# One slot more in a ring of weight chunks, one split buffer fewer of each kind

## The chip, the cores and the metric

The kernel runs on one core of one Trainium2 chip. The metric is the device time of a launch in microseconds, median over the runs. One further execution was taken with the hardware profiler, and every row shown here comes from that one.

## The reference, cut to what matters

One layer of a decoder trunk on 512 tokens of width 1024, in float32. A token mixer (three groups of heads: a convolution, a gated recurrence, chunked linear attention) is followed by a mixture of 16 experts in 4 groups: each token takes the best group and in it the best two experts. The change touches only how the weights of the experts are held, so only that part is shown.

```python
def hier_moe(h, w_rg, b_rg, w_re, b_re, w_gate, w_up, w_down):
    ...
    for g in range(N_GROUPS):
        a = jnp.einsum("bsd,edf->bsef", h, w_gate[g])
        up = jnp.einsum("bsd,edf->bsef", h, w_up[g])
        hid = jax.nn.silu(a) * up * comb[:, :, g, :, None]
        y = y + jnp.einsum("bsef,efd->bsd", hid, w_down[g])
    return y

def reference(...):
    ...
        x = x + gt1 * token_mix(h, ...)
        h = rms_norm(x, g_ffn[l]) * (1.0 + sc2) + sh2
        x = x + gt2 * hier_moe(h, ...)
    return rms_norm(x, g_final)
```

With `D_MODEL = 1024` and `D_EXPERT = 512`, each expert has three matrices of 2 MB, so the 16 experts have 96 MB, and all of it is read.

## The kernel before

The first half of the time goes to the token mixer and the routing. Behind it stands the unit loop over the experts, about 262 to 525 us of the profile. The kernel gathers the tokens of an expert (at most 128), multiplies, and adds the results back to the rows in memory.

**Units.** Eight units (0 to 7) hold one expert each, with up to 128 tokens; the code calls them `alone(u)`. Four units (8 to 11) hold two experts each, with up to 64 tokens apiece, in the two halves of the array. In the order of the program, unit u does its gate product, the transposes of the hidden rows of unit u-1, its up product, the transposes of the gathered rows of unit u+1, and then the down product of unit u-1 (`whole`), whose result is scaled by `gt2` (tile `ye`) and scattered.

**Chunks.** Each matrix is loaded in two chunks of 1 MB (`load_chunk`, line 964), 96 chunks in all, in the order of use: gate, up, and the down of the unit before. A chunk lives in a slot of the ring: chunk `i` in slot `i % nring`. `nring` is 17: 13 slots from pools that are opened as earlier stages end, and four of the pool `ring2`, which takes the place of the mixer's last tiles. A load waits for its slot to be free of the chunk `nring` back, and for the load three before it, so that three are on the way at a time. All loads go through SP's queue, in order. Nine chunks are loaded while the mixer still runs, three more behind its projections, four as the routing ends, and `for i in range(HELD + 1, nring)` loads those that are left ahead of the unit loop.

**Splits.** In the single-expert units the product is made in three parts of reduced precision. A chunk is taken in two halves, called quarters (of a matrix). For each quarter ScalarE casts the weights (line 87, tile `mh`), and VectorE subtracts the cast from the weights (line 88, tile `ml`):

```python
        hi = mw.tile([P, k // 4, 4096 // k], F32R, tag="mh", name=f"mh_{name}{s}")
        lo = mw.tile([P, k // 4, 4096 // k], F32R, tag="ml", name=f"ml_{name}{s}")
        split(hi, lo, raw[:, s * (k // 4):(s + 1) * (k // 4), :])
        if s:
            load_chunk(i + nring)
```

TensorE then does two triples per quarter in `mm3`: line 82 (cast weights, cast rows), line 83 (remainder of the weights), line 84 (cast weights, remainder of the rows). The pool `mw` has three buffers of `mh` and three of `ml`, 4 KB a partition each. A new tile in a buffer waits for every reader of the old one. When the second quarter of a chunk is split, the slot is free and the next load is traced. In the down product the last quarter is used as it is, unsplit (line 1449, four matmuls), in all single-expert units but 3 and 7 (`full(u)`).

The paired units use the chunks straight from the ring (lines 1412 and 1458), with no split; a slot is free once its matmuls are done.

**Order.** The program is written in the order above, and at build time the framework makes from it one list per engine, by priority and its own estimates of when an operand is there. In the trace the lists mix neighbouring units: a one-hot product of a later unit stands between two subtractions, transposes of gathered rows between two quarters of a down. At run time each engine goes through its list in order and waits where it must.

**The tail.** When the chunks are through, `slot` goes on in the same ring for seven more tiles (two with split results, four with rows of the output, one with the final scale).

Of the kernel before, what the change touches and what calls it, by code (L numbers as in the profile page):

```python
# [42 lines left out]
EARLY = 12  # L43
# [3 lines left out]
def trunk_kernel(  # L47
# [105 lines left out]
    rings = []  # L153

    def add_ring(n, name, side="right"):
        pool = ctx.enter_context(tc.tile_pool(name=name, bufs=n, side=side, reuse_waits="tile"))
        rings.extend([pool] * n)
        return pool
# [785 lines left out]
                              for s in range(2) for c in cols_of(n))  # L944
    picked = {}
    raws = {}
    nring = len(rings) + 4

    loads = []

# [4 lines left out]
    def load_chunk(i, *first):  # L955
        if i >= len(chunks):
            return
        w, c, k, s, _, name = chunks[i]
        raw = rings[i % nring].tile([P, k // 2, 4096 // k], F32, tag="raw", name=f"raw_{name}")
        if c >= NS and c not in picked:  # L960
            picked[c] = nc.values_load(ranked[0:1, c - NS:c - NS + 1], engines=[mybir.EngineType.SP],
                                       min_val=NS, max_val=NE - 1)
        src = w[c:c + 1] if c < NS else w[bass.ds(picked[c], 1)]
        d = nc.sync.dma_start(raw, src.rearrange("e (p k) n -> p (e k) n", p=P)[:, s * (k // 2):(s + 1) * (k // 2), :])

        if len(loads) >= AHEAD:
            after(d, loads[-AHEAD])
        for other in first:
            after(d, other)
        loads.append(d)  # L970
        raws[i] = raw

    for i in range(nring - 8):
        load_chunk(i)

    def yres(i, half, ps):
# [48 lines left out]
    def route(i):  # L1025
        route_half(i, 1)
        nc.sync.dma_start(xo_dram[i * P:(i + 1) * P, :], xt[i])
        junk = late.tile([P, D], BF16, tag="junk2", bufs=1, name=f"junk2{i}")
        nc.scalar.activation(junk, xt[i], AF.Square, accum_out=ss2[:, i:i + 1])
        rstd_of(ss2[:, i:i + 1], ss2[:, i:i + 1], D)  # L1030
        pl2 = small(f"pl2{i}")
        for hf in range(2):
            nc.tensor.matmul(pl2[:, 0:20], pls[i, hf], sel, start=(hf == 0), stop=(hf == 1))
        nc.vector.scalar_tensor_tensor(lg[:, i, :], pl2[:, 0:20], ss2[:, i:i + 1], lgc, ALU.mult, ALU.add)
# [13 lines left out]
    for i in range(2):  # L1048
        yres(i, 1, py[i])
    py = project((2, 3), [lambda i=i: [route_half(n, 0) for n in (i, i + 1)] for i in (0, 2)]  # L1050
                 + [lambda i=i: route(i) for i in (0, 1)])
    for i in range(nring - 8, EARLY):
        load_chunk(i)
    for i in (0, 1):
        rows(i)
# [11 lines left out]
    for g in gat:  # L1067
        nc.gpsimd.memset(g, 0.0)
    lts.close()
    add_ring(4, "ring2", side="left")  # L1070
    mw = ctx.enter_context(tc.tile_pool(name="mw", bufs=3, reuse_waits="tile"))
    hpool = ctx.enter_context(tc.tile_pool(name="hot", bufs=4, reuse_waits="tile"))

    shalf = hpool.tile([P, 2 * (NU - NS - NB)], U32, bufs=1, name="shalf")
# [591 lines left out]
```

## Time and profile before

| | us |
|---|---|
| median of 3 runs | 544.43 |
| the three runs | 543.29 to 544.66 |
| the profiled execution, own time | 542.79 |
| its span (first to last instruction) | 541.1 |
| busy in the span: TensorE | 509.2 |
| VectorE | 362.6 |
| ScalarE | 248.4 |
| GpSimd | 90.4 |

The span is what the trace shows; the 1.7 us between it and the execution's own time lie around it. Engines are called PE (TensorE), PEld (its weight loads), DVE (VectorE), ACT (ScalarE), POOL (GpSimd) and SP, whose queue issues the loads. Busy time is a sum over the whole span: a stage in which an engine is full and one in which it is idle come out as one share. Matmuls are pipelined, so one lasts longer in the record than the distance to the next.

### The profile page before, as it was taken

To read this page: it belongs to the slowest core of one execution; us is meant where nothing else is said; L and a number is where in the kernel's file an instruction comes from. 1 tells how busy PE (TensorE), PEld (TensorE's weight loads), DVE (VectorE), ACT (ScalarE), POOL (GpSimd) and SP (SyncE) were. 2 spreads that over 40 slices of the span, in tenths; PEclk is the share of its full clock that TensorE was granted. 3 is DMA by queue.
4 is the path that set the end of the run, shared out by engine and by line. 5 is a ranking of instruction groups with operands and counts; after the bars stand their busy time and mean duration, and the time that the engine had idled before them with its cause. 6 is when DMAs were issued, how large, how long until landed. Compare 5 with 4: busy or idle time off the path is not lost.

```text
span 541.1 us, 7963 instructions
## 1 busy us (share of the span) xinstructions
PE 509.2 (94%) x2835; PEld 344.8 (64%) x2835; DVE 362.6 (67%) x654; ACT 248.4 (46%) x397; POOL 90.4 (17%) x126
## 2 busy tenths in 40 slices
PE   8999999999989999997889999999999999999891
PEld 7766766677657887766668777787876443342341
DVE  4544499999988747448799999999897121020227
ACT  5432587496126533334457768676774110000103
POOL 3311424000025100104110220120222010211002
PEclk9999999999999999996699999999999999999996
DMA  8995978748818399379899899999999999999963
GB/s 284 302 345 160 273 259 269 249 164 303 274 60 303 124 395 421 115 265 313 297 329 327 316 377 364 353 365 382 353 373 377 367 403 366 402 368 375 391 252 155
DMA packets 54304, 164.58 MB, mean 304 GB/s; under 512 B 12181, under 2 KB 30881, under 8 KB 39926
## 3 DMA queue, kind: packets, MB, share of 16 engines
q1 hardware_dynamic: 50710, 156.36, 78.9%
q0 software_dynamic: 3552, 7.69, 5.4%
q8 instruction: 23, 0.38, 0.3%
q14 instruction: 19, 0.16, 0.1%
HBM read 156.35 MB, written 12.62 MB: 312 GB/s over the span
## 4 chain that ended last, share of the span: by engine, by line
PE 28%; DMA 16%; DVE 5%; issue 1%; ACT 0%; POOL 0%; POOLq 0%; DVEq 0%; SPq 0%
DMA raw_u<-in_w_up_dram 7%; DMA raw_d<-in_w_down_dram 6%; DMA raw_g<-in_w_gate_dram 3%; PE pga L84 2%; PE pga L83 2%; PE pga L82 2%; PE pup L83 2%; PE pup L84 2%; PE pup L82 2%; PE pd L82 2%; PE pd L1449 2%; PE pd L83 2%; PE pd L84 2%; PE pd L1458 2%; PE pgt L1381 2%; PE pga L1412 1%
## 5 line engine op out<-in xcount | busy, mean ns | idle before, releaser
L507 DVE SCALAR_TENSOR_TENSOR cacc<-upad,vt,cacc 128x512 f32<-128x512 f32 x60 | 43.1, 755 | 0.1
L1536 DVE SCALAR_TENSOR_TENSOR sact<-pup,swt,sact 128x512 f32<-128x512 f32 x12 | 8.9, 745 | 50.1 <-PE pup L1412 50.1
L88 DVE TENSOR_TENSOR ml_u<-raw_u,mh_u 128x1024 fp32r<-128x1024 f32 x32 | 39.1, 1224 | 3.9 <-ACT mh_u L87 3.7
L87 ACT CAST mh_g<-raw_g 128x1024 fp32r<-128x1024 f32 x32 | 33.4, 1051 | 16.9 <-PE pga L84 12.3
L88 DVE TENSOR_TENSOR ml_g<-raw_g,mh_g 128x1024 fp32r<-128x1024 f32 x32 | 38.3, 1219 | 1.3 <-ACT mh_g L87 1.1
L87 ACT CAST mh_u<-raw_u 128x1024 fp32r<-128x1024 f32 x32 | 33.6, 1049 | 11.6 <-PE pga L84 9.4
L1458 PE MATMUL pd<-raw_d,ht 128*64 128x512 f32 x128 | 35.0, 600 | 1.5 <-DMA raw_d<-in_w_down_dram 1.5
L88 DVE TENSOR_TENSOR ml_d<-raw_d,mh_d 128x1024 fp32r<-128x1024 f32 x26 | 31.7, 1222 | 4.0 <-ACT mh_d L87 3.6
L1140 POOL DMA_INDIRECT gat<-h_rows,sidx x12 | 13.5, 1122 | 121.1 <-PE pgt L1381 68.9
L87 ACT CAST mh_d<-raw_d 128x1024 fp32r<-128x1024 f32 x26 | 27.3, 1049 | 8.1 <-PE pup L84 6.1
L1412 PE MATMUL pup<-raw_u,xh 128*64 128x512 f32 x128 | 29.4, 595 | 1.2 <-DMA raw_u<-in_w_up_dram 1.2
L1486 DVE TENSOR_TENSOR ye<-pd,gt 128x512 f32<-128x512 f32 x22 | 15.0, 690 | 21.8 <-PE pd L1458 20.3
L1412 PE MATMUL pga<-raw_g,xh 128*64 128x512 f32 x128 | 28.3, 594 | 0.0
L82 PE MATMUL pga<-mh_g,xh 128*128 128x512 f32 x64 | 27.4, 428 | 0.5 <-ACT xh L87 0.5
L83 PE MATMUL pup<-ml_u,xh 128*128 128x512 f32 x64 | 25.6, 400 | 1.6 <-DVE ml_u L88 1.5
L83 PE MATMUL pga<-ml_g,xh 128*128 128x512 f32 x64 | 26.1, 408 | 1.0 <-DVE ml_g L88 1.0
L84 PE MATMUL pga<-mh_g,xl 128*128 128x512 f32 x64 | 25.5, 399 | 0.4 <-DVE xl L88 0.4
L82 PE MATMUL pup<-mh_u,xh 128*128 128x512 f32 x64 | 25.8, 403 | 0.0
L84 PE MATMUL pup<-mh_u,xl 128*128 128x512 f32 x64 | 25.2, 394 | 0.0
L1458 PEld LDWEIGHTS pd<-raw_d,ht 128*64 128x64 f32 x128 | 10.8, 136 | 21.4 <-issue 16.8
L1084 POOL DMA_INDIRECT xo_rows<-ye,sidx x8 | 17.1, 2138 | 36.8 <-DVE ye L1486 36.8
L1424 ACT COPY ht<-pht 128x512 f32<-128x512 f32 x4 | 2.3, 586 | 43.0 <-PE pht L1420 43.0
(405 smaller groups left out, 1270.1 us busy)
## 6 DMA issues: line engine op xcount, KB each, us to landing
raw_g<-in_w_gate_dram SPq DMA_DIRECT2D x32, 1024.0 KB
raw_u<-in_w_up_dram SPq DMA_DIRECT2D x32, 1024.0 KB
raw_d<-in_w_down_dram SPq DMA_DIRECT2D x32, 1024.0 KB
wb<-in_w_ada_dram SPq DMA_DIRECT2D x16, 1024.0 KB
wa<-in_w_ada_dram SPq DMA_DIRECT2D x8, 512.0 KB
wa<-in_w_ada_dram SPq DMA_DIRECT2D x4, 1024.0 KB
raw_o<-in_w_out_dram SPq DMA_DIRECT2D x8, 512.0 KB
xin<-in_x_dram SPq DMA_DIRECT2D x4, 512.0 KB
```

The lines of the kernel that those rows point to most:

```text
L82: nc.tensor.matmul(ps, lh, rh, start=start, stop=False)
L83: nc.tensor.matmul(ps, lh, rl, start=False, stop=False)
L84: nc.tensor.matmul(ps, ll, rh, start=False, stop=stop)
L87: one = nc.scalar.copy(hi, src)
L88: two = nc.vector.tensor_tensor(lo, src, hi.bitcast(F32), ALU.subtract)
L507: nc.vector.scalar_tensor_tensor(cacc[:, h, :], upad[:, h, t:t + T], w, cacc[:, h, :], ALU.mult, ALU.add)
L1084: nc.gpsimd.indirect_dma_start(out=xo_dram, out_offset=bass.IndirectOffsetOnAxis(ap=si, axis=0), in_=y, in_offset=None, bounds_check=T - 1 ...
L1140: return g, nc.gpsimd.indirect_dma_start(out=g, out_offset=None, in_=h2_dram, in_offset=bass.IndirectOffsetOnAxis(ap=sidx[:, e:e + 1], axi ...
L1381: nc.tensor.transpose(pt[:, kk * P:(kk + 1) * P], gv[:, :, k], ident)
L1412: nc.tensor.matmul(ps[rows_of(a)], xh[:, k, rows_of(a)], raws[used[0] + a][:, kk, :], start=(k == 0), stop=(k == KD - 1))
L1458: nc.tensor.matmul(ps[hf][rows_of(a)], ht[:, k, rows_of(a)], raws[used[0] + k // 2 * 2 + a][:, k % 2, cols(hf)], start=(k == 0), stop=(k = ...
L1486: nc.vector.tensor_tensor(y[:, cols], ps[hf], gt2[:, cols], ALU.mult)
```

## The change

The ring gets an eighteenth slot: `ring2` has five slots, not four. Two numbers that are worked out from `nring` are set so that the same nine and three chunks as before are loaded ahead of the routing. The room of 8 KB a partition comes from the pool `mw`: two buffers of `mh` and two of `ml`, not three.

```diff
-    nring = len(rings) + 4
+    nring = len(rings) + 5
...
-    for i in range(nring - 8):
+    for i in range(nring - 9):
         load_chunk(i)
...
-    for i in range(nring - 8, EARLY):
+    for i in range(nring - 9, EARLY):
         load_chunk(i)
...
-    add_ring(4, "ring2", side="left")
-    mw = ctx.enter_context(tc.tile_pool(name="mw", bufs=3, reuse_waits="tile"))
+    add_ring(5, "ring2", side="left")
+    mw = ctx.enter_context(tc.tile_pool(name="mw", bufs=2, reuse_waits="tile"))
```

## Rows read from the trace of the kernel before

**Rows 1.** The page, busy time, share and instructions of each engine.

```profile
PE 509.2 (94%) x2835; PEld 344.8 (64%) x2835; DVE 362.6 (67%) x654; ACT 248.4 (46%) x397; POOL 90.4 (17%) x126
```

**Rows 2.** Windows: length, busy PE, PEld, DVE, ACT, POOL, granted clock, DMA share, GB/s.

```profile
300.00:310.00 10.00, 10.00 (x44) 7.66 (x43) 9.27 (x10) 6.88 (x9) 2.36 (x1) 1.00 0.88 304
...
440.00:450.00 10.00, 10.00 (x50) 3.48 (x46) 0.00 (x0) 1.08 (x2) 0.00 (x0) 1.00 1.01 372
...
490.00:500.00 10.00, 8.75 (x40) 2.77 (x36) 0.18 (x1) 0.60 (x1) 1.55 (x1) 1.00 1.02 374
...
500.00:510.00 10.00, 8.95 (x34) 3.18 (x34) 1.35 (x5) 0.59 (x1) 0.00 (x0) 1.00 1.02 378
```

**Rows 3.** The chain that ended last: start us, us, what.

```profile
299.76 1.72 PE pd L1449 x4
...
352.52 0.90 PE pgt L1381 x8
...
413.74 1.72 PE pd L1449 x4
...
504.47 7.80 DMA raw_d<-in_w_down_dram
```

**Rows 4.** Waits of SP's queue, 283 to 415 us: us in total, times, longest.

```profile
SPq L964 <- DMA raw_g<-in_w_gate_dram: 26.7, 13, 3.8
...
SPq L964 <- DVE ml_g L88: 10.9, 8, 2.5
```

**Rows 5.** Waits of SP's queue, 414 to 418 us.

```profile
SPq L964 <- PE pd L1449: 2.5, 1, 2.5
```

**Rows 6.** Groups by form, 283 to 415 us: busy us, mean ns of one.

```profile
L84 PE MATMUL pga<-mh_g,xl 128*128 128x512 f32 x56 | 22.2, 397 | 0.4 <-DVE xl L88 0.4
...
L82 PE MATMUL pd<-mh_d,hh 128*128 128x512 f32 x44 | 17.8, 411 | 0.0
...
L1486 DVE TENSOR_TENSOR ye<-pd,gt 128x512 f32<-128x512 f32 x13 | 8.8, 689 | 0.4 <-PE pd L1449 0.2
...
L1536 DVE SCALAR_TENSOR_TENSOR sact<-pup,swt,sact 128x512 f32<-128x512 f32 x7 | 5.2, 742 | 0.0
...
L1535 ACT ACTIVATE sact<-pga 128x512 f32<-128x512 f32 x7 | 4.2, 601 | 0.0
...
L1226 DVE TENSOR_TENSOR ohs<-iota,pos 128x512 bf16<-128x512 f32 x4 | 2.7, 687 | 0.0
```

**Rows 7.** Timeline, 273 to 277 and 323 to 325 us: start us, us, engine, what.

```profile
273.10 1.22 DVE L88 TENSOR_TENSOR ml_u<-raw_u,mh_u 128x1024 fp32r<-128x1024 f32 x1
...
274.37 0.50 PE L83 MATMUL pup<-ml_u,xh 128*128 128x512 f32 x1 [1.54 <-DVE ml_u L88]
...
275.42 0.40 PE L84 MATMUL pup<-mh_u,xl 128*128 128x512 f32 x1
...
275.85 1.05 ACT L87 CAST mh_u<-raw_u 128x1024 fp32r<-128x1024 f32 x1 [1.97 <-PE pup L84]
...
276.93 1.23 DVE L88 TENSOR_TENSOR ml_u<-raw_u,mh_u 128x1024 fp32r<-128x1024 f32 x1
...
323.04 0.39 PE L82 MATMUL pga<-mh_g,xh 128*128 128x512 f32 x1
...
324.44 0.39 PE L82 MATMUL pga<-mh_g,xh 128*128 128x512 f32 x1
```

**Rows 8.** Waits of ScalarE's casts, 283 to 415 us: us in total, times, longest.

```profile
ACT mh_g L87 <- PE pga L84: 12.3, 7, 2.1
...
ACT mh_u L87 <- PE pga L84: 7.4, 20, 0.7
...
ACT mh_d L87 <- PE pup L84: 6.1, 17, 0.7
```

**Rows 9.** Issues of loads, size of one.

```profile
raw_g<-in_w_gate_dram SPq DMA_DIRECT2D x32, 1024.0 KB
```

**Rows 10.** Window of 2 us in unit 0, columns as in rows 2.

```profile
272.00:274.00 2.00, 0.83 (x11) 0.36 (x9) 2.00 (x3) 1.54 (x2) 0.00 (x0) 1.00 0.96 360
```

## The prediction

> **What bounds the kernel now.** I read the page first [rows 1]: TensorE is busy 94% of the span. That is an average over stages, so the windows come next [rows 2]. In the stage of the whole-unit experts (units 1 to 7, about 283 to 415 us) TensorE is busy for the whole of 10 us at the full granted clock, VectorE for 9.27 of them, and the transfers for 88%: three resources close to full at once. In the stage of the paired experts, behind 415 us, VectorE is nearly idle and the transfers run at a share of about 1 (372 GB/s); TensorE is full there too but for the last 20 us, in which it waits some 2.3 us. The chain of waits [rows 3] goes through matmuls up to 415.5 us and in the paired stage through transfers of weights, the last until 512.3 us. So the end is set by the weight stream and by TensorE together, and both enter the paired stage when the first stage lets them.
>
> That the stream can't run on by itself is in the waits of SP's queue. In the first stage [rows 4] a load most often waits for an earlier one (13 times for a gate load, 26.7 us), but 8 times for ml_g, the subtraction that ends the use of a gate chunk. Where the stages meet [rows 5] it waits for line 1449's matmuls, 2.5 us: there the ring is full, and a later end of unit 7 holds back the stream.
>
> The groups by form [rows 6] give the work of that stage: 56 matmuls of line 84 for gate, as many for up and 44 for down, two to a quarter, so 28 + 28 + 22 = 78 quarters. The groups of line 1449 (1.72 us for four) that end the downs of units 0 and 6 start at 299.76 and 413.74 us [rows 3], six periods apart: 19.0 us a unit. Quarters follow each other in 1.40 us (323.04 to 324.44, [rows 7]). Eleven of them make 15.4, line 1449 1.7, transposes and one-hot products the rest, about 1.8.
>
> **The change, part by part.**
>
> *Two split buffers of each kind, not three.* Follow one set of buffers in the timeline [rows 7]. A subtraction on VectorE starts at 273.10 and takes 1.22, to 274.32; the second matmul of that quarter, which needs it, starts at 274.37, 0.05 later. The sixth starts at 275.42 and ends at 275.82. ScalarE starts the cast that uses the set next at 275.85, named as released by that matmul; it takes 1.05, and its subtraction starts at 276.93, 0.03 behind its end, and takes 1.23. Once round: 0.03 + 1.05 + 0.03 + 1.23 + 0.05 + 1.45 (second matmul's start to sixth's end) = 3.84 us. A set must go round once in as many quarters as there are sets. With three, TensorE's pace gives 3 x 1.40 = 4.20: 0.36 to spare. The waits say how near the limit that is: 44 of the 78 casts (7 + 20 + 17) waited for just this last matmul [rows 8]. With two, the pace gives 2.80 and the loop still wants 3.84, so the loop becomes the bound: 1.92 us a quarter, not 1.40. What hid the 2.4 us of cast and subtraction was two further quarters of matmuls (2.80); one (1.40) doesn't.
>
> Behind the waiting cast on ScalarE stand the copy of the transposed hidden rows, the SiLU and the casts of the gathered rows; VectorE's product of SiLU and up waits for those, and TensorE's transposes and downs for that.
>
> Now one unit. *Lower end*: 11 x 1.92 = 21.1; line 1449 makes its pair of quarters 2.80 + 1.72 = 4.52, 0.7 over the loop; the other TensorE work fits gaps of 0.52. 21.8 us, 2.8 more than now. The one unit of the seven whose down is split in all four quarters (down 3) wants 12 x 1.92 = 23.0, 4.0 more. Sum 6 x 2.8 + 4.0 = 20.8. *With today's order kept* I carried the loop through a unit by hand. VectorE does the scaled output (2 x 0.69) ahead of the third gate subtraction, a one-hot (0.69) ahead of the fourth, the product with up (0.74) ahead of the third down; ScalarE does copy and SiLU (0.60) ahead of the last up cast; TensorE does eight transposes (0.90, [rows 3]) ahead of the second down quarter. Counted from the end of line 1449, the second matmuls fall at 0.23, 1.63, 3.96, 5.88, 7.85, 9.71, 11.57, 13.71, 15.51, 17.80, 19.81, and the next unit's first at 23.03: 22.8 us, 3.9 more than the 18.9 that the same count gives for now. For the full unit it gives 23.8, 5.0 more. Sum 6 x 3.9 + 5.0 = 28.4. *Upper end*: of VectorE's 5 us of other work in a unit about 1 falls on the loop in this count; if half did, a unit takes 24.3, and seven 5.4 each, 38. The build orders each engine's list anew, so a better fit may take some of the 28.4 back. I take **26**, nearer to the order seen than to the floor.
>
> *Units 0 and 7.* In unit 0 (262 to 282 us) VectorE also sorts the tables and is the bound; the loop's gap lies partly under that. Zero to 4 us; I take **2**. Two quarters of down 7 fall into the paired stage, and wait about 1 us each there; zero where the stream is the bound, 2 where TensorE is; I take **1**.
>
> *The eighteenth slot.* The loads ahead of the unit loop are the same and one more; from then on a load waits for the chunk 18 back. Where the stages meet, the stream is one chunk further. A chunk is 1024 KB [rows 9]; at 372 GB/s that is 2.8 us less to move in the paired stage. Nothing, if TensorE fills that time by itself; at most about 2.8, since TensorE has but 2.3 us of idle time there [rows 2] and little behind. I take **-2.8**. Slack of the transfers in the slower first stage gives no more: a load needs a slot.
>
> *The rest.* The loads' kinds and their order stay, and so does the computation; the tail takes its tiles from ring slots in rotation, one slot earlier than now. Nothing, with the last stage's transfers as cover; if a tail tile came behind the last down, a us or two.
>
> Sum: 26 + 2 + 1 - 2.8 = 26.2. The profiled execution took 542.8 us (its span 541.1 and 1.7 around it): 569.0. The median of the runs shown stands 1.6 above that execution, so I say **570 us**.
>
> **The rivals.**
>
> *A. Two sets are enough, and the slot gains.* The split of the next quarter goes on under the matmuls of this one, and the stream's lead of a chunk comes out at the end: 542.8 - 2.8 = 540, or 542 as a median. It decides if the loop is under 2.80 us. For it: ScalarE and VectorE have idle time in each quarter. Against it: cast and subtraction alone take 2.28, which leaves 0.5 for the matmuls between. The Trainium skill, in Trainium Kernel Development and Optimization, Best Practices, says to double-buffer for performance. Read as "two will do" it gives this rival's time; rows 7 and 8 speak against it. 4%.
>
> *B. The build interleaves better.* If all other TensorE work (3.5 us a unit) and all of VectorE's fits the gaps, a unit takes 21.1: 7 x 2.1 - 2.8 = 12 more, or 556. If matmuls of other units stepped into the gaps too, some 3 to 10 more. For it: today's lists mix units. Against: with two sets only two quarters are ready at a time, of whichever unit. 10%, with a tenth of that inside 0.3%.
>
> *C. The clock falls.* With a gap in every quarter the granted clock may go to 0.5, the 1.2 GHz level. Matmuls would then start 0.47 apart, and a unit take some 35 us; over half of the stage that is 43 us more, about 613 with the rest. Against it: at 272 to 274 us TensorE was busy for 0.83 of 2 us and the granted clock was 1.00 [rows 10]. The Trainium skill, TensorE: Matmul & The Clock Gate, A second HAM failure mode, tells of short idles between groups of matmuls that make the clock swing; row 10 shows such a stall without it. 4%.
>
> **How the numbers follow.** My forecast, +12 to +39 by the bounds above, has 82%; B 10% and A 4% lie below it, C 4% above. The range for 8 in 10 goes from the case in which the gaps take up all other work (556) to the upper end (38 + 4 - 2.8 = 39, 584). Within 0.3% (1.6 us, about what a measurement here can tell from no change): 3%. Faster: 3%, all of it A. Slower: 94%.
>
> **What would show it.** Line 1449's groups 22 to 23 us apart; nearly all 78 casts released by a matmul; TensorE idle for about half a us ahead of most second matmuls, released by the subtraction; the transfers' share in that stage near 0.8, with SP waiting for subtractions; the paired stage as long as now or up to 3 us shorter; the clock at 1.00. I'd be wrong if line 1449's groups stayed 19 us apart (A), or if the paired stage were 10 us or more shorter and gave the loss back.

## The result and the profile after

| | us |
|---|---|
| before, median of 3 runs | 544.43 |
| after, median of 3 runs | 567.85 (567.34 to 568.54) |
| ratio, 95% interval | 1.0441 [1.0408, 1.0473] |
| profiled execution after, own time | 567.34 |
| its span | 565.4, before 541.1 |

Slower by 4.4%, 23.4 us on the median and 24.3 us on the span; 570 us was forecast, between 556 and 584. The chain of waits after answers to [rows 3]: start us, us, what.

```profile
304.25 1.72 PE pd L1449 x4
...
395.20 1.72 PE pd L1449 x4
...
436.05 1.00 PE pga L1412 x2
...
437.72 1.01 PE pga L1412 x4
...
441.24 1.72 PE pd L1449 x4
...
528.21 8.35 DMA raw_d<-in_w_down_dram
```

The first and the last group of line 1449 stand at 304.25 and 441.24 us, 137.0 us apart where it was 114.0: a unit takes 22.8 us, not 19.0. The first group is 4.5 us late, the last 27.5, the end of the span 24.3. So all of the loss is made up to 441 us, and 3.2 us come back in the paired stage. The windows of the two stages, before and then after (columns as in [rows 2]):

```profile
283.00:415.00 132.00, 131.93 (x670) 103.09 (x669) 122.76 (x144) 95.19 (x111) 21.56 (x13) 1.00 0.97 357
415.00:512.00 97.00, 94.51 (x442) 36.64 (x440) 16.81 (x32) 8.72 (x15) 10.43 (x7) 1.00 1.00 381
```

```profile
283.00:443.00 160.00, 148.08 (x679) 102.23 (x680) 123.12 (x144) 95.88 (x112) 20.11 (x14) 1.00 0.89 304
443.00:536.00 93.00, 93.00 (x434) 35.90 (x434) 17.84 (x32) 9.99 (x16) 10.44 (x7) 1.00 0.99 376
```

VectorE does the same 123 us of work in the first stage, over 160 us where it was 132; no engine is full there, and the transfers fall from a share of 0.97 to 0.89. The paired stage is as before, but TensorE no longer has idle time in it. What the first stage waits for is in the timeline, which answers to [rows 7]:

```profile
287.07 1.05 ACT L87 CAST mh_g<-raw_g 128x1024 fp32r<-128x1024 f32 x1 [1.24 <-PE pga L84]
...
288.15 1.23 DVE L88 TENSOR_TENSOR ml_g<-raw_g,mh_g 128x1024 fp32r<-128x1024 f32 x1 [0.91 <-ACT mh_g L87]
...
289.43 0.50 PE L83 MATMUL pga<-ml_g,xh 128*128 128x512 f32 x1
...
290.47 0.40 PE L84 MATMUL pga<-mh_g,xl 128*128 128x512 f32 x1
...
290.91 1.05 ACT L87 CAST mh_u<-raw_u 128x1024 fp32r<-128x1024 f32 x1 [1.38 <-PE pga L84]
...
293.27 0.50 PE L83 MATMUL pup<-ml_u,xh 128*128 128x512 f32 x1 [0.33 <-DVE ml_u L88]
...
294.74 1.05 ACT L87 CAST mh_u<-raw_u 128x1024 fp32r<-128x1024 f32 x1 [0.94 <-PE pup L84]
```

Read it as a circle: cast at 287.07, its subtraction at 288.15, the second matmul at 289.43, the sixth at 290.47, and the next cast on that set at 290.91, released by it: 3.84 us. The next turn ends at 294.74, 3.83 us on. Each step of the circle starts 0.03 to 0.05 us behind the end of the step before it. The groups of waits say how often an engine stood still for that, between 283 and 442 us (us in total, times, longest):

```profile
PEld pup L83 <- DVE ml_u L88: 16.3, 25, 1.1
ACT mh_g L87 <- PE pga L84: 14.6, 13, 2.1
...
ACT mh_u L87 <- PE pga L84: 10.7, 13, 1.4
ACT mh_g L87 <- PE pd L84: 9.6, 12, 1.6
ACT mh_u L87 <- PE pup L84: 9.2, 11, 1.2
...
PEld pd L83 <- DVE ml_d L88: 6.1, 12, 1.0
ACT mh_d L87 <- PE pup L84: 5.0, 7, 0.9
...
ACT mh_d L87 <- PE pd L84: 4.3, 3, 2.8
PEld pga L83 <- DVE ml_g L88: 4.0, 10, 0.8
```

59 of 78 casts wait for a sixth matmul, 53.4 us in all. That count by itself says little: with three sets 55 casts did (the 44 of [rows 8] and two groups that aren't shown there), for 29.7 us:

```profile
ACT mh_g L87 <- PE pd L84: 3.2, 9, 0.6
...
ACT mh_d L87 <- PE pd L84: 0.7, 2, 0.3
```

What is new is on TensorE. Before 47 of the 78 quarters its weight load waits for a subtraction, 26.4 us, near the 27.5 us that are lost up to the last group; with three sets that were 3 waits and 0.9 us. (While a load waits, earlier matmuls still run: the matmuls themselves stand idle for a subtraction 30 times, 10.2 us.) On SP's queue, in the same stretch, the loads that in [rows 4] mostly waited for an earlier load now wait for subtractions:

```profile
SPq L964 <- DVE ml_u L88: 45.1, 14, 3.7
SPq L964 <- DVE ml_g L88: 28.5, 10, 4.1
SPq L964 <- DVE ml_d L88: 27.4, 12, 4.4
...
SPq L964 <- DMA raw_g<-in_w_gate_dram: 1.1, 2, 0.9
```

The ring is full nearly throughout: an eighteenth slot in it holds a chunk that nobody is ready to use.

### The profile page after: what moved, and what is told of

Read it like the earlier page. It is cut to its first block, busy times and chain, and to the rows that moved or that the text cites. A ratio compares the mean times of both kernels' runs of the same rounds, so it can differ in the third digit from the quotient of the medians.

```text
span 565.4 us, 7966 instructions
## 1 busy us (share of the span) xinstructions
PE 523.2 (93%) x2835; PEld 341.5 (60%) x2835; DVE 363.1 (64%) x654; ACT 248.8 (44%) x397; POOL 87.6 (15%) x126
## 4 chain that ended last, share of the span: by engine, by line
PE 30%; DVE 11%; ACT 5%; DMA 5%; issue 1%; POOL 0%; POOLq 0%; DVEq 0%; SPq 0%; ACTq 0%
PE pga L1412 4%; PE pd L1458 4%; PE pup L1412 4%; DMA raw_d<-in_w_down_dram 3%; DVE ml_u L88 3%; DVE ml_d L88 3%; DVE ml_g L88 2%; PE pga L83 2%; PE pd L83 2%; PE pup L83 2%; ACT mh_u L87 2%; PE pd L1449 2%; PE pga L84 2%; ACT mh_g L87 2%; PE pd L84 2%; PE pgt L1381 2%
## 5 line engine op out<-in xcount | busy, mean ns | idle before, releaser
L83 PE MATMUL pup<-ml_u,xh 128*128 128x512 f32 x64 | 28.4, 444 | 7.5 <-DVE ml_u L88 7.4
L1084 POOL DMA_INDIRECT xo_rows<-ye,sidx x8 | 15.7, 1958 | 117.2 <-DVE ye L1486 117.2
L1412 PE MATMUL pga<-raw_g,xh 128*64 128x512 f32 x128 | 30.6, 595 | 0.0
L83 PE MATMUL pga<-ml_g,xh 128*128 128x512 f32 x64 | 28.0, 437 | 2.5 <-DVE ml_g L88 2.1
L83 PE MATMUL pd<-ml_d,hh 128*128 128x512 f32 x52 | 22.0, 423 | 2.4 <-DVE ml_d L88 2.2
L83 PEld LDWEIGHTS pup<-ml_u,xh 128*128 128x128 f32 x64 | 12.0, 187 | 19.3 <-DVE ml_u L88 17.7
```

The lines of the kernel that those rows point to most:

```text
L83: nc.tensor.matmul(ps, lh, rl, start=False, stop=False)
L1084: nc.gpsimd.indirect_dma_start(out=xo_dram, out_offset=bass.IndirectOffsetOnAxis(ap=si, axis=0), in_=y, in_offset=None, bounds_check=T - 1 ...
L1412: nc.tensor.matmul(ps[rows_of(a)], xh[:, k, rows_of(a)], raws[used[0] + a][:, kk, :], start=(k == 0), stop=(k == KD - 1))
```

## The experiments

Each ratio below is against the kernel before as measured beside that run; its median was 544.03, 544.69 or 545.66 us.

**Is it the split buffers or the slot?** The two parts of the change, apart. First the buffers alone:

```diff
-    mw = ctx.enter_context(tc.tile_pool(name="mw", bufs=3, reuse_waits="tile"))
+    mw = ctx.enter_context(tc.tile_pool(name="mw", bufs=2, reuse_waits="tile"))
```

> The cut of the split buffers alone: two of each kind, the ring stays at 17. Loop theory (a set of buffers must go round in 3.84 us while TensorE gives it 2.80): unit 7's last line 1449 about 27 us later than before, as with the whole change, and the ratio 1.044 to 1.049, 568 to 571 us: 2.8 us above the whole change if the slot is worth its chunk, nothing above it if TensorE fills the paired stage by itself. Rival (the ring's new slot, with its place or its rotation, makes the loss): about 544 us.

Measured: 569.37 us, ratio 1.0467 [1.0444, 1.0489]. The whole loss is there without the slot. In its chain of waits:

```profile
440.88 1.72 PE pd L1449 x4
```

The last group comes at 440.88, with the whole change at 441.24; the span ends at 567.1 and 565.4. So from the last group on it is 126.2 us with 17 slots, 124.2 with 18, and 127.4 before. With two sets, the slot is worth about 2.0 us on these executions; on the medians it is 1.5, and the intervals of the two ratios overlap.

Then the slot alone, downwards: 16 slots, three sets.

```diff
-    nring = len(rings) + 4
+    nring = len(rings) + 3
...
-    add_ring(4, "ring2", side="left")
+    add_ring(3, "ring2", side="left")
```

The two loops ahead of the routing count from `nring - 7`, so that they load the same chunks.

> A slot fewer than before, 16, with three buffers of each kind. If a slot is worth the transfer of a chunk at the meeting of the stages, 2.8 us more: 547 us. If the paired stage is bound by TensorE's own work, or the planner shifts other work, 0 to 1.5 us: 544 to 546. If the first stage starves for weights, more than 5 us.

Measured: 544.70 us, ratio 1.0010 [0.9990, 1.0030]. No difference that can be told from none. The first stage doesn't starve with 16 slots.

**Which buffer of the pair?** The loop as I read it goes through the cast's buffer. Two kernels with 17 slots, one buffer fewer of one kind each:

```diff
-        hi = mw.tile([P, k // 4, 4096 // k], F32R, tag="mh", name=f"mh_{name}{s}")
+        hi = mw.tile([P, k // 4, 4096 // k], F32R, tag="mh", bufs=2, name=f"mh_{name}{s}")
```

> Two cast buffers, three remainder buffers, ring of 17. Loop theory: the cast's buffer is held until the sixth matmul of its quarter, and the way round from there goes through cast, subtraction and the matmuls, 3.84 us, whatever the remainders have: as slow as two of each, 566 to 572 us. Rival (the number of buffers in all counts): half of the loss, about 556 us.

Measured: 570.33 us, ratio 1.0487 [1.0465, 1.0509]. One cast buffer costs the whole loss. The other way round, `bufs=2` on the tile `ml` alone:

> Three cast buffers, two remainder buffers, ring of 17. Loop theory: a remainder's buffer is held until the fifth matmul, and the way round from there is the subtraction alone and the matmuls: 0.03 + 1.23 + 0.05 + 1.21 (second matmul's start to the fifth's end) = 2.52 us, under the 2.80 of TensorE's pace; so no loss, 543 to 547 us. Rival (buffers in all): about 556 us.

Measured: 545.23 us, ratio 1.0021 [1.0004, 1.0038]. Either gives up 4 KB a partition; the one costs 26 us and the other 1. The chain of the first and then of the second:

```profile
440.40 1.72 PE pd L1449 x4
```

```profile
415.08 1.72 PE pd L1449 x4
```

It isn't the number of buffers that counts but how long each is held, and by whom. A remainder is free after the fifth matmul and is written by VectorE alone, a turn of 2.52 us by the durations. A cast is held to the sixth, and VectorE must have read it before TensorE can go on: 3.84. The 2.52 is only worked out: no run here makes the remainder's turn the bound.

**Can the loop be made shorter?** Then two sets would do. The same six matmuls of a quarter in another order (gate and up shown; the down in the same manner): first the four that read the cast, then the two that read the remainder.

```diff
                     for kk in range(2):
                         k = s * 2 + kk
-                        mm3(ps, xh[:, k, :], xl[:, k, :], hi[:, kk, :], lo[:, kk, :], k == 0, k == KD - 1)
+                        nc.tensor.matmul(ps, xh[:, k, :], hi[:, kk, :], start=(k == 0), stop=False)
+                        nc.tensor.matmul(ps, xl[:, k, :], hi[:, kk, :], start=False, stop=False)
+                    for kk in range(2):
+                        k = s * 2 + kk
+                        nc.tensor.matmul(ps, xh[:, k, :], lo[:, kk, :], start=False, stop=(k == KD - 1))
```

With the whole change (two sets, 18 slots):

> The whole change, and the six matmuls of a quarter in another order: the four that read the casts first, the two that read the remainders last (the sum in PSUM is taken in that order). Loop theory: the casts are free after the fourth matmul and the remainders are needed only from the fifth. From the fourth's end 0.03 + 1.05 + 0.03 + 1.23 + 0.05 = 2.39 us to the fifth of the next quarter on the set, which TensorE's pace reaches after 2.80 - 0.17 = 2.63: no wait in the steady state, 0.24 to spare. So most of the 23 us come back, 543 to 550 us, the upper part if the other work of VectorE and ScalarE uses up the 0.24. Rival (two sets are too few whatever the order, since cast, subtraction and matmuls follow each other): 560 us or more.

Measured: 541.86 us, ratio 0.9960 [0.9936, 0.9983]. Its chain (line 1449 is line 1453 there):

```profile
300.39 1.72 PE pd L1453 x4
...
414.02 1.72 PE pd L1453 x4
```

The last group is back at 414.02 us, with two sets of buffers, and the groups are 18.9 us apart. All but 0.3 of the 27.5 us are gone by the order, so the loss was the time for which the cast is held. The control, that order with three sets and 17 slots:

> The kernel before with that order of matmuls alone: control. TensorE's work is the same and three sets have slack in either order: 542 to 546 us by the loop theory. A change of more than 3 us would say that the order acts by itself (weight loads, PSUM), and the run with two sets would have to be read against this one.

Measured: 542.34 us, ratio 0.9965 [0.9943, 0.9987]: the order gains about 2 us by itself. In its chain:

```profile
298.82 1.72 PE pd L1453 x4
...
412.21 1.72 PE pd L1453 x4
```

The last group stands 1.5 us earlier than before, and 0.9 of that is there at the first group; what makes up those 1.5 us is not shown. Read against this control, two sets still cost 1.8 us up to the last group (414.02).

The control also settles what the waits of casts can tell. By the turn worked out above it has more slack than the kernel before, yet 57 of its casts wait for a matmul, 29.9 us, as 55 did for 29.7. A cast that runs ahead of TensorE has to wait for it at some point, however much slack there is. And the order with two sets and 17 slots:

> Two sets, the new order of matmuls, 17 slots: beside the same with 18 slots it gives the slot's worth when the first stage is at TensorE's pace. If a slot gives its chunk, 2.8 us above that run; if TensorE's work fills the paired stage, 0 to 1.5 us above.

Measured: 544.75 us, ratio 1.0005 [0.9988, 1.0023]. In its chain:

```profile
413.37 1.72 PE pd L1453 x4
```

Beside the run with 18 slots, on the same chip, that makes the slot worth 2.9 us on the medians and 2.4 by the ratios, about the transfer of one chunk. Beside the control, with three sets and 17 slots too, two sets cost 2.4 us on the medians (2.2 by the ratios, whose intervals just fail to meet): 1.2 of it up to the last group, the rest behind it, and why is not shown.

**Is it a loop with a length?** One set, 17 slots, the old order (`bufs=1` in the pool `mw`).

> One set of split buffers, ring of 17: the loop's length measured by itself. Loop theory: a set goes round once a quarter, so a quarter takes 3.84 us and TensorE's other work fits beside cast and subtraction. A unit with eleven quarters takes 42.2 us, down 3's with twelve 46.1, so line 1449's first and last groups stand 5 x 42.2 + 46.1 = 257 us apart (before: 114); units 0 and 1 have 19 quarters, 73 us from 263, and the paired stage stays at about 124 us from the last group on: 263 + 73 + 257 + 124 = 717, between 700 and 735 us. Rival (the loss with two sets is VectorE's and ScalarE's work falling out of step, not a loop with a length): well under that, 600 to 660 us.

Measured: 787.16 us, ratio 1.4432 [1.4389, 1.4474]. Far above both. Its timeline, casts of successive quarters in two stretches:

```profile
322.16 1.04 ACT L87 CAST mh_u<-raw_u 128x1024 fp32r<-128x1024 f32 x1 [3.35 <-PE pup L84]
...
327.05 1.04 ACT L87 CAST mh_u<-raw_u 128x1024 fp32r<-128x1024 f32 x1 [3.85 <-PE pup L84]
...
407.14 1.04 ACT L87 CAST mh_g<-raw_g 128x1024 fp32r<-128x1024 f32 x1 [1.96 <-PE pga L84]
...
410.96 1.04 ACT L87 CAST mh_g<-raw_g 128x1024 fp32r<-128x1024 f32 x1 [2.78 <-PE pga L84]
```

and windows of it, columns as in [rows 2]:

```profile
308.00:310.00 2.00, 0.87 (x4) 0.24 (x2) 0.39 (x1) 1.04 (x1) 0.00 (x0) 1.00 0.98 246
...
322.00:324.00 2.00, 0.86 (x2) 0.28 (x1) 0.76 (x1) 1.04 (x1) 0.00 (x0) 0.50 0.00 0
```

At 407 us a turn takes 3.82 us, as the loop theory has it; the granted clock of that turn is 1.00. At 322 us it takes 4.89: the granted clock is at 0.50 there, the 1.2 GHz level. It goes back and forth; over the stage the groups of line 1449 are 51.7 us apart, not the 42.8 of the expectation (257 / 6):

```profile
350.60 3.08 PE pd L1449 x4
...
401.82 3.07 PE pd L1449 x4
...
660.82 1.72 PE pd L1449 x4
```

Between the first two of these groups the granted clock has a mean of 0.63, so about three quarters of the time are at the lower level. Eleven turns with that mix come to 11 x (3.82 + 0.74 x 1.07) = 50.7 us by estimate, and the two groups are 51.2 apart. So the length of the loop is borne out, the forecast time is not: it left out the clock, which with two sets had stayed at 1.00. The Trainium skill, TensorE: Matmul & The Clock Gate, A second HAM failure mode, tells of short idles between groups of matmuls (in its case with PSUM banks taken in turn) that do this. With one set, in which TensorE waits for the cast and again for the subtraction in each turn, the trace shows such a swing; with two it doesn't.

**The slot, paid for elsewhere.** Three cast buffers, two remainder buffers, 18 slots; the other 4 KB come from the scaled output (`ye`, one buffer, not two), and one tile of the branch for overfull experts, which doesn't run on this input, shares another's place.

> Eighteen slots, paid with one remainder buffer (4 KB) and one of the two buffers of the scaled output (4 KB), casts at three. Loop theory: no loss from the remainders (as with 17 slots); the scaled output's one buffer is free when its scatter has landed, some 11 us before the next is written. So 542 to 546 us; by the slot's worth between 16 and 17 (0.5 us) and between 17 and 18 with two sets (1.5 us) not measurably faster than before. If a slot is worth 2.8 us once the first stage isn't slowed: 541 to 542.

Measured: 543.96 us, ratio 0.9985 [0.9962, 1.0007]. Not measurably faster than before. The kernel that differs by the slot and its payment is the one with three cast and two remainder buffers and 17 slots (1.0021 [1.0004, 1.0038], on another chip): beside that it is 2.0 us less, with intervals that just overlap. The 11 us of slack in the expectation are not borne out: a scatter takes 10.9 us (median) to land, and from there to the next write some 5 us are left, still enough. The same with the new order of matmuls, and, beside it, the new order with two sets and 18 slots again:

> All that the runs so far point to: matmuls in the new order, three cast and two remainder buffers, eighteen slots, one buffer for the scaled output. From 542.3 us (new order, three of each, 17 slots) less the slot's worth, 1.5 to 2.9 us: 539.5 to 541 us. If the slot's worth is only there when two sets slow the first stage, 542.

> The kernel of the first run with the new order (two sets, 18 slots) again, on the same chip as the run before this one, to compare the two: 541 to 543 us; if the third cast buffer is worth anything in the new order, up to 2.4 us above that run.

Measured: 541.75 us, ratio 0.9948 [0.9929, 0.9967], and 542.01 us, ratio 0.9939 [0.9920, 0.9957]. The first was expected a little lower, and the two are the same: in the new order and with 18 slots a third cast buffer shows no gain, unlike the third set with 17. The second is the same kernel as the first run with the new order, whose ratio was 0.9960: so much do two measurements differ. The change of this study plus the new order is faster than both kernels it began from, by 0.4 to 0.6% against the kernel before; so, within the intervals, is the new order with everything else left as it was (0.35%).

What a slot is worth is known only roughly. From the last group of line 1449 to the end of the span, the profiles with the first stage at TensorE's pace have 126.9 us with 16 slots, 127.2 to 128.6 with 17 (four profiles), and 125.7 to 126.4 with 18 (four profiles). The 2.9 us above is the widest pair of these; the means of 17 and 18 are 1.6 apart, and 16 is no worse than 17.

## Why the prediction was right

*The loop.* Predicted 3.84 us a turn from the durations in a kernel in which it wasn't yet the bound; measured 3.84 and 3.83. It passed three tests: alone, with one set, it takes 3.82 at the full clock; with the other kind of buffer cut instead there is next to no loss (0.2%); and with the order of readers changed the loss is gone. What the prediction took for a sign of the limit, casts that wait for the last matmul, was none: it named 44 of 55 such waits, and the control has 57.

*The unit.* Carried by hand with the old order: 22.8 us, and 23.8 for the one with four split down quarters; 5 x 22.8 + 23.8 = 137.8 between the first and last group of line 1449. Measured 137.0. In time added, six units by hand are 5 x 3.9 + 5.0 = 24.5, and 23.0 was measured. The groups between show units of 22.4 to 22.6 us, and 23.4 for the last, which also holds six matmuls of unit 8 (below). I took 2.4 us off the sum of seven for a better fit of the new lists, and about that much came: with unit 0 the hand count is 30.4, measured 27.5. The build did order anew (transposes of a unit in twos and fours in gaps); that this is what gave the difference was not tried.

*Unit 0.* The first group of line 1449 is 4.5 us late; 2 for unit 0 and 3.9 for unit 1 had been counted, 5.9. Together, unit 0 and the seven: 27.5 measured, 28 predicted. How the 4.5 us divide between the two units can't be told from the groups.

*The paired stage.* Predicted -1.8 (-2.8 for the slot, +1 for down 7), measured -3.2. By the run with 17 slots, 2.0 of it is the slot; the other 1.2 has the size of the six matmuls of unit 8's gate product that the build put into the gaps of the down of unit 6, ahead of the last group (at 436.05 and 437.72 us, 6 x 0.22 = 1.3). Part of the 27.5 us is then work of the next stage: the last unit is 0.9 us longer than the regular ones before it. I had said of such matmuls that only two quarters are ready at a time; they need none. That is what rival B had right, and it was small. That these six make the 1.2 is worked out, not tried. The extra us for down 7 can't be told apart in this (all four of its quarters lie in the paired stage, not two). So the forecast of this part was right in sign and 1.4 us short in size. With the 0.5 us too much in the first stage, and the 1.6 us added for the median, which lies only 0.5 above the profiled execution after, that is the 2 us by which 570 is too high. The 26 in the sum was picked between a floor of 20.8 and the hand count of 28.4, not worked out: that it fell so close is in part luck.

*The rest.* Too bold in two places that should have shown the mechanism: not nearly all casts but 59 of 78 wait for a matmul, hardly more than before, and the transfers' share in the first stage falls to 0.89, not 0.8. The 0.88 that the prediction started from was one window of 10 us; the stage before had 0.97. TensorE's waits for the subtraction, about half a us each (26.4 us in 47), came as forecast. The clock stayed at 1.00, as [rows 10] had let me expect.

*The rivals.* A (two sets are enough) fails in the old order and nearly holds in the new: 1.0005 with 17 slots, where three sets in that order have 0.9965. The sentence of the Trainium skill (Trainium Kernel Development and Optimization, Best Practices) on double-buffering speaks of transfers under compute; read as the prediction reads it, for buffers between engines, it is wrong here (1.0467) or nearly right by the order in which six matmuls read their operands. C (the clock falls) did not happen with two sets and did with one.

## What to carry to other kernels

How many buffers a stage needs is the time once round (from the last reader's end through every engine that refills it, to that reader again), divided by the pace of the bounding engine; here 3.84 / 1.40 = 2.7, so three. The durations in the kernel before gave that though TensorE hardly stood still there; how often the refilling engine waited did not. Before giving memory to buffers, see which reader holds them last, and whether it can read earlier: here an order of six matmuls did nearly what a third cast buffer of 4 KB a partition did. And a deeper ring paid little here: the eighteenth slot 1 to 3 us in the pairs of runs, about the transfer of a chunk at most, with the first stage slowed or not, and the seventeenth nothing that could be told from none.

## What the runs showed of the hardware that I had not expected

The granted clock can swing in a steady loop: with one set of buffers it went between 1.00 and 0.50 in a stage whose work is the same six matmuls from quarter to quarter, and a turn took 3.82 or 4.89 us. With two sets, TensorE's weight loads waiting for 26.4 us in 47 places of a stage of 160 us, it stayed at 1.00 throughout that stage.
